# Cumulative sums of stick-breaking attention: six fp32 products for each head become six fp32r products on a split operand

## The chip, the cores and the metric

The kernel runs on one NeuronCore of a Trainium2 chip. The metric is the time of one execution on the device in microseconds (us). Its engines are named as in the profile: PE is TensorE (matmuls), PEld is TensorE's weight load, DVE is VectorE, ACT is ScalarE, POOL is GpSimd and SP is SyncE, whose queue issues most of the transfers.

## The reference, cut to what matters

The model is two transformer blocks on 256 tokens and 16 meta tokens. The change is inside the attention of the second block, in its eight stick-breaking heads. For each query the logarithm of the attention weight of a key is a log-sigmoid plus the sum of another log-sigmoid over all later keys, a reversed cumulative sum:

```
def stick_breaking_block(q, k, v, qpos, kpos):
    z = jnp.einsum('bhqd,bhkd->bhqk', q, k).astype(jnp.float32) * (SB_HEAD_DIM ** -0.5)
    causal = kpos[None, :] < qpos[:, None]
    u = jnp.where(causal, jax.nn.log_sigmoid(-z), 0.0)
    rest = lax.cumsum(u, axis=3, reverse=True) - u
    log_a = jax.nn.log_sigmoid(z) + rest
    a = jnp.where(causal, jnp.exp(log_a), 0.0)
    return jnp.einsum('bhqk,bhkd->bhqd', a.astype(v.dtype), v)
```

## The kernel before, in words

Nearly all of the work is a stream of weight units, each a 128x1024 piece of some weight matrix. A unit is loaded by SP (L130), and split into two fp32r tiles: ACT copies it to `hi` with rounding (L152) and DVE writes the remainder to `lo` (L154). `mm_w` then makes 24 products for it on PE (L183 to L185): high by high, high by low, low by high, for eight slices. Three `hi` and three `lo` buffers exist, so ACT may write the next `hi` when PE has done with the unit three before.

The second block begins, at 934 us of the span, with a transition: the sums of the expert layer are read from PSUM, normalised, transposed (`to_feats`) and become the operand `xT2` of all that follows. Then the eight stick-breaking heads run, from about 955 to 1053 us, and after them the eight heads of the differential attention. For each head `hd` three weight units give queries, keys and values (`ps_sq`, `ps_sk`, `ps_svT`). Between them, by hand, the steps of the generator `stick` are issued; each `yield` in it lets one more weight unit go by. So the attention of a head is spread over the units of the next two heads:

- Step 1: `z` is the product of keys and queries. Keys stand on the 128 partitions, in three tiles; queries stand in the columns. Of the 256 queries key tile 0 needs all, tile 1 only the last 144, tile 2 only the last 16, which makes 256 + 144 + 16 = 416 columns side by side in one PSUM bank. DVE adds the mask (L998), ACT makes the softplus in three steps (L1000 to L1002), and DVE ends it in `e` (L1003).
- Step 2, one unit later: the values are transposed (L985) and copied by ACT (L986).
- Step 3, two units later: the cumulative sums `S`, from `e`, on PE (L1011). For each key tile a product with the triangle `tri` sums the later keys of the same tile, and products with `ones` add all of the later tiles: tile 0 gets 256 columns from itself, 144 from tile 1 and 16 from tile 2; tile 1 gets 144 and 16; tile 2 gets 16. That makes six matmuls in fp32 and 592 columns. Each fp32 matmul stands in the trace as two records, with a weight load each. DVE subtracts `S` from `z` (L1013), and ACT takes the exponential (L1014).
- Step 4, two units later: the product with the values, `po` (L1019), which ACT and DVE split into `osb` (L1020, L1021).

The order on PE and SP is the program's. The order on ACT, DVE and POOL is set by a scheduler, by priority; each engine then runs its instructions strictly in that order.

Of the kernel before, what the change touches and what calls it, by code (L numbers as in the profile page):

```python
# [9 lines left out]
F32 = mybir.dt.float32  # L10
F32R = mybir.dt.float32r
I32 = mybir.dt.int32
U32 = mybir.dt.uint32
AF = mybir.ActivationFunctionType
ALU = mybir.AluOpType
# [4 lines left out]
P = 128  # L20
# [32 lines left out]
def two_blocks(ctx, tc, x, feats, vecs, w_in, w_out, w_q, keys, u, v, final_g, meta2, w_in2, lams, w_gate,  # L53
               w_br_sb, w_br_df, w_out2, w_fg, w_fu, w_fd, final_g2, gains, out):
    nc = tc.nc
# [9 lines left out]
    def phase(name):  # L65
        st = ExitStack()
        pool = st.enter_context(tc.tile_pool(name=name, bufs=1, reuse_waits="tile"))
        return st, pool

    def mm_tile(name):  # L70
        return pmm.tile([P, 512], F32, tag="mm", name=name)
# [3 lines left out]
    def at_tile(name):  # L75
        turn[0] += 1
        return pacc.tile([P, 512], F32, tag=f"a{turn[0] % 4}", name=name)
# [252 lines left out]
    ones = const.tile([P, P], F32, tag="ones", name="ones")  # L330
# [473 lines left out]
    for hd in range(NH):  # L804
        kt = pr.tile([P, 2, P], F32, tag="kt", name=f"kt{hd}", bufs=2)
        nc.sync.dma_start(kt, keys[:, 2 * hd:2 * hd + 2, :])
        qT = []
        for half in range(2):
            ps = mm_tile(f"q{hd}{half}")
# [118 lines left out]
    QN = [T - q0 for q0 in Q0]  # L928
    QO = [0, QN[0], QN[0] + QN[1]]
    NQ = sum(QN)  # L930
# [5 lines left out]
    s_sb, psb = phase("psb")  # L936
# [5 lines left out]
    for kt in range(3):  # L942
        o = mneg[:, QO[kt]:QO[kt] + QN[kt]]
        nc.gpsimd.affine_select(o, o, [[1, QN[kt]]], ALU.is_gt, -BIG, base=NM + Q0[kt] - kt * P, channel_multiplier=-1)
    tri = psb.tile([P, P], F32, tag="tri", name="tri")
    nc.gpsimd.affine_select(tri, ones, [[-1, P]], ALU.is_ge, 0.0, base=0, channel_multiplier=1)


    KN = [NM + P, L]
# [31 lines left out]
    def value(name, tag, vt):  # L981
        ps = at_tile(f"pv_{name}")
        o = psb.tile([P, 3, P], F32, tag=tag, name=name, bufs=2)
        for kt in range(3):
            nc.tensor.transpose(ps[:, kt * P:(kt + 1) * P], vt[:, kt * P:(kt + 1) * P], ident)  # L985
        nc.scalar.activation(o, ps[:, :KP].rearrange("p (a b) -> p a b", a=3), AF.Copy)  # L986
        return o

    def qcols(kt, j=None):
        j = kt if j is None else j  # L990
        return slice(QO[kt] + Q0[j] - Q0[kt], QO[kt] + QN[kt])

    def stick(hd, q, k, vT):
        pz = at_tile(f"z{hd}")
        for kt in range(3):
            nc.tensor.matmul(pz[:, qcols(kt)], k[:, kt * P:(kt + 1) * P], q[:, Q0[kt]:], start=True, stop=True)
        z = psb.tile([P, NQ], F32, tag="z", name=f"zs{hd}", bufs=2)
        nc.vector.tensor_tensor(z, pz[:, :NQ], mneg, op=ALU.add)  # L998
        e = psb.tile([P, NQ], F32, tag="e", name=f"e{hd}", bufs=2)
        nc.scalar.activation(e, z, AF.Abs)  # L1000
        nc.scalar.activation(e, e, AF.Exp, scale=-1.0)
        nc.scalar.activation(e, e, AF.Ln, bias=1.0)  # L1002
        nc.vector.scalar_tensor_tensor(e, z, 0.0, e, op0=ALU.max, op1=ALU.add)  # L1003
        yield
        vt = value(f"sv{hd}", "sv", vT)
        yield
        yield
        ps = at_tile(f"S{hd}")
        for kt in range(3):
            for j in range(kt, 3):  # L1010
                nc.tensor.matmul(ps[:, qcols(kt, j)], tri if j == kt else ones, e[:, qcols(j)],  # L1011
                                 start=(j == kt), stop=(j == 2))
        nc.vector.tensor_tensor(z, z, ps[:, :NQ], op=ALU.subtract)  # L1013
        nc.scalar.activation(z, z, AF.Exp)  # L1014
        yield
        yield
        po = at_tile(f"po{hd}")
        for kt in range(3):
            nc.tensor.matmul(po[:, Q0[kt]:T], vt[:, kt, :], z[:, qcols(kt)], start=(kt == 0), stop=(kt == 2))  # L1019
        nc.scalar.activation(osb[0][:, hd, :], po[:, :T], AF.Copy)  # L1020
        nc.vector.tensor_tensor(osb[1][:, hd, :], po[:, :T], osb[0][:, hd, :].bitcast(F32), op=ALU.subtract)  # L1021
# [73 lines left out]
    for hd in range(NH):  # L1095
        q = feat(f"sq{hd}", hd, "sq", QS, float(P) ** -0.5) if hd != 1 else ahead
        if hd > 1:
            q = q()
            advance()
        k = feat(f"sk{hd}", hd, "k", FULL, spare=(hd == 1))  # L1100
        if hd == 1:
            q = q()
            advance()
        if hd > 0:
            k = k()
            advance()
        else:
            with tc.high_priority(offset=20):
                cols = x2_norm()
        vT = feat(f"svT{hd}", hd, "vT", FULL)  # L1110
        if hd == 0:
            ahead = feat("sq1", 1, "sq", QS, float(P) ** -0.5)
            with first():
                across(pb, cols, rsb[:, QS], "rsb")
            tc.keep_in_program_order(nc.scalar.preload_act_table_set("natural_log_exp_and_others"))
            q, k = q(), k()
        running.append(stick(hd, q, k, vT()))
        if hd > 0:
            advance()
        if hd == 0:  # L1120
            with queued([latest["hi"], latest["lo"]]):
                small_parts()
# [8 lines left out]
    for m in range(16):  # L1131
        ps = mm_tile(f"g{m}")
# [13 lines left out]
    for m in range(KC):  # L1146
        ps = mm_tile(f"ysb{m}")
# [3 lines left out]
    for m in range(KC + 1):  # L1151
        if m < KC:
            ps = mm_tile(f"ydf{m}")
# [144 lines left out]
```

## Time and profile before

| | us |
|---|---|
| median of three runs | 1450.63 |
| lowest and highest | 1447.94 and 1456.06 |
| the profiled execution | 1450.2 |
| its span in the trace | 1448.2 |
| PE busy in the span | 1435.2 (99%) |
| DVE busy | 1049.0 (72%) |
| ACT busy | 743.4 (51%) |
| the stretch of the stick-breaking heads | 955 to 1053 |

The profiled execution took 2.0 us more than its span, for what lies around it. A busy PE in the table is a PE with a matmul in its pipeline; since matmuls overlap, their real cost is the distance from the start of one to the start of the next, and not their duration. Where a question is about one stage, the rows of that stage count, not the shares over the whole span.

### The profile page before, as it was taken

How to read it: one execution, taken by the hardware profiler on the slowest of the kernel's cores; microseconds unless marked ns; L12 is line 12 of the kernel's file. 1: busy time of each engine (PE TensorE's matmuls, PEld its weight loads, DVE VectorE, ACT ScalarE, POOL GpSimd, SP SyncE). 2: the span in 40 equal slices, each digit the busy share in tenths (PEclk: the TensorE clock that was granted, in tenths of full speed). 3: DMA queues.
4: the chain of work that ended last, by engine and by line, in shares of the span. 5: the costliest groups of instructions: out<-in, count | busy, mean ns of one | idle time of the engine just before them, and what ended most of it. 6: DMA issues, size and time to landing. Idle time of an engine off the chain costs nothing.

```text
span 1448.2 us, 25653 instructions
## 1 busy us (share of the span) xinstructions
PE 1435.2 (99%) x10150; PEld 1338.4 (92%) x10150; DVE 1049.0 (72%) x1887; ACT 743.4 (51%) x1236; POOL 15.5 (1%) x35
## 2 busy tenths in 40 slices
PE   9999999999999999999999999999999999999998
PEld 8988999999999999888888888899999999899997
DVE  8998789884998999655555565675577776765666
ACT  7556544544444444544444444564455764554444
POOL 0010000000000000000000000100000000000000
PEclk9999999999999999999999999999999999999999
DMA  7526656665444444566666676553434466556563
GB/s 245 197 80 197 195 179 181 183 200 184 153 132 146 147 141 139 183 194 192 194 196 192 192 254 191 182 181 117 131 117 132 131 183 183 173 185 192 186 195 102
DMA packets 69816, 248.96 MB, mean 172 GB/s; under 512 B 7744, under 2 KB 9152, under 8 KB 69696
## 3 DMA queue, kind: packets, MB, share of 16 engines
q1 hardware_dynamic: 68256, 242.61, 53.6%
q0 software_dynamic: 1152, 4.19, 0.9%
q8 instruction: 79, 1.29, 0.4%
q10 hardware_dynamic: 288, 0.52, 0.1%
q14 instruction: 41, 0.34, 0.1%
HBM read 245.20 MB, written 2.10 MB: 171 GB/s over the span
## 4 chain that ended last, share of the span: by engine, by line
PE 92%; DVE 5%; ACT 1%; issue 1%; DMA 0%; POOL 0%; SPq 0%; DVEq 0%; POOLq 0%; ACTq 0%
PE v L197 8%; PE v L199 8%; PE v L198 8%; PE u L183 7%; PE u L185 7%; PE u L184 7%; PE gp L753 4%; PE fg L184 1%; PE fg L185 1%; PE fg L183 1%; PE fu L183 1%; PE fu L185 1%; PE fu L184 1%; PE fd L199 1%; PE fd L198 1%; PE fd L197 1%
## 5 line engine op out<-in xcount | busy, mean ns | idle before, releaser
L154 DVE TENSOR_TENSOR lo<-raw,hi 128x1024 fp32r<-128x1024 f32 x453 | 552.1, 1224 | 244.0 <-ACT hi L152 241.7
L152 ACT ACTIVATE hi<-raw 128x1024 fp32r<-128x1024 f32 x453 | 477.0, 1058 | 420.4 <-PE u L184 119.8
L183 PE MATMUL u<-hThi,hi 128*128 128x256 f32 x1024 | 295.6, 289 | 0.0
L185 PE MATMUL u<-hThi,lo 128*128 128x256 f32 x1024 | 284.9, 278 | 0.6 <-DVE lo L154 0.6
L184 PE MATMUL u<-hTlo,hi 128*128 128x256 f32 x1024 | 284.8, 278 | 0.0
L198 PE MATMUL v<-lo,w_hi 128*128 128x512 f32 x512 | 199.3, 389 | 0.0
L199 PE MATMUL v<-hi,w_lo 128*128 128x512 f32 x512 | 199.2, 389 | 0.0
L197 PE MATMUL v<-hi,w_hi 128*128 128x512 f32 x512 | 199.2, 389 | 0.0
L185 PEld LDWEIGHTS u<-hThi,lo 128*128 128x128 f32 x1024 | 193.3, 189 | 1.2 <-DVE lo L154 1.2
L184 PEld LDWEIGHTS u<-hTlo,hi 128*128 128x128 f32 x1024 | 192.9, 188 | 0.0
L183 PEld LDWEIGHTS u<-hThi,hi 128*128 128x128 f32 x1024 | 192.7, 188 | 0.0
L198 PEld LDWEIGHTS v<-lo,w_hi 128*128 128x128 f32 x512 | 96.1, 188 | 20.2 <-DVE lo L154 0.2
L199 PEld LDWEIGHTS v<-hi,w_lo 128*128 128x128 f32 x512 | 96.1, 188 | 20.1
L197 PEld LDWEIGHTS v<-hi,w_hi 128*128 128x128 f32 x512 | 96.1, 188 | 19.6
L753 PE MATMUL gp<-ga,gb 128*128 128x128 f32 x512 | 74.9, 274 | 0.0
L753 PEld LDWEIGHTS gp<-ga,gb 128*128 128x128 f32 x512 | 66.2, 191 | 0.0
L851 ACT ACTIVATE w_hi<-ewa 128x512 fp32r<-128x512 f32 x48 | 30.4, 634 | 65.8 <-PE v L198 65.8
L853 DVE TENSOR_TENSOR w_lo<-ewa,w_hi 128x512 fp32r<-128x512 f32 x48 | 33.2, 693 | 38.6 <-ACT w_hi L851 38.6
L184 PE MATMUL fg<-hTlo,hi 128*128 128x256 f32 x176 | 48.9, 278 | 0.2 <-DVE hTlo L257 0.2
L183 PE MATMUL fg<-hThi,hi 128*128 128x256 f32 x176 | 48.9, 278 | 0.1
L185 PE MATMUL fg<-hThi,lo 128*128 128x256 f32 x176 | 48.9, 278 | 0.0
L183 PE MATMUL fu<-hThi,hi 128*128 128x256 f32 x176 | 48.7, 277 | 0.0
(417 smaller groups left out, 2957.7 us busy)
## 6 DMA issues: line engine op xcount, KB each, us to landing
raw<-in_u_dram SPq DMA_DIRECT2D x128, 512.0 KB, 3.6
raw<-in_v_dram SPq DMA_DIRECT2D x128, 512.0 KB, 3.6
raw<-in_w_in_dram SPq DMA_DIRECT2D x67, 512.0 KB, 3.6
raw<-in_w_fg_dram SPq DMA_DIRECT2D x22, 512.0 KB, 4.1
raw<-in_w_fu_dram SPq DMA_DIRECT2D x22, 512.0 KB, 3.5
raw<-in_w_fd_dram SPq DMA_DIRECT2D x22, 512.0 KB, 4.5
raw<-in_w_out_dram SPq DMA_DIRECT2D x16, 512.0 KB, 3.7
raw<-in_w_q_dram SPq DMA_DIRECT2D x16, 512.0 KB, 4.4
```

The costliest lines, as they stand in the source:

```text
L152: latest["hi"] = nc.scalar.activation(hi, loaded[i], AF.Copy)
L154: latest["lo"] = nc.vector.tensor_tensor(lo, loaded[i], hi.bitcast(F32), op=ALU.subtract)
L183: nc.tensor.matmul(ps, hi[:, ks], ahi[:, k, cols], start=(k == 0), stop=False)
L184: nc.tensor.matmul(ps, hi[:, ks], alo[:, k, cols], start=False, stop=False)
L185: nc.tensor.matmul(ps, lo[:, ks], ahi[:, k, cols], start=False, stop=(k == KC - 1))
L197: nc.tensor.matmul(ps, ahi[:, ts], hi[:, bs], start=first and n == 0, stop=False)
L198: nc.tensor.matmul(ps, ahi[:, ts], lo[:, bs], start=False, stop=False)
L199: nc.tensor.matmul(ps, alo[:, ts], hi[:, bs], start=False, stop=end)
L753: nc.tensor.matmul(p3[:, :, i], b[:, i, :], a[:, i, :], start=True, stop=True)
L851: nc.scalar.activation(hi, a, AF.Copy)
L853: nc.vector.tensor_tensor(lo, a, hi.bitcast(F32), op=ALU.subtract)
```

## The change

The operand `e` of the cumulative sums is split in two fp32r tiles: `ehi` is a rounded copy made by ACT, `elo` is the remainder, made by DVE. The constants `tri` and `ones` are copied once to fp32r by ACT (their values 0 and 1 are exact there). The six fp32 products of a head become six fp32r products, three for `ehi` and the same three for `elo`: one with the triangle over all 416 columns, which does the three tiles' own sums; one with `ones` that adds tile 1 to tile 0 (144 columns); and one with `ones` that adds tile 2 to both tile 0 and tile 1, by reading its 16 columns twice and writing them to two places of the bank (2 x 16 columns).

```
+    tri_r = psb.tile([P, P], F32R, tag="tri_r", name="tri_r")
+    nc.scalar.activation(tri_r, tri, AF.Copy)
+    ones_r = psb.tile([P, P], F32R, tag="ones_r", name="ones_r")
+    nc.scalar.activation(ones_r, ones, AF.Copy)
...
         nc.vector.scalar_tensor_tensor(e, z, 0.0, e, op0=ALU.max, op1=ALU.add)
+        ehi = psb.tile([P, NQ], F32R, tag="ehi", name=f"ehi{hd}", bufs=2)
+        nc.scalar.activation(ehi, e, AF.Copy)
+        elo = psb.tile([P, NQ], F32R, tag="elo", name=f"elo{hd}", bufs=2)
+        nc.vector.tensor_tensor(elo, e, ehi.bitcast(F32), op=ALU.subtract)
         yield
...
         ps = at_tile(f"S{hd}")
-        for kt in range(3):
-            for j in range(kt, 3):
-                nc.tensor.matmul(ps[:, qcols(kt, j)], tri if j == kt else ones, e[:, qcols(j)],
-                                 start=(j == kt), stop=(j == 2))
+
+
+        c0, c1 = qcols(0, 2).start, qcols(1, 2).start
+        o = 512 - 2 * (c1 - c0)
+        both = ps[:, o:].rearrange("p (a b) -> p a b", a=2)[:, :, c0 - o:c0 - o + QN[2]]
+        for half in (ehi, elo):
+            third = half[:, qcols(2)].unsqueeze(1).broadcast_to((P, 2, QN[2]))
+            nc.tensor.matmul(ps[:, :NQ], tri_r, half, start=(half is ehi), stop=False)
+            nc.tensor.matmul(ps[:, qcols(0, 1)], ones_r, half[:, qcols(1)], start=False, stop=False)
+            nc.tensor.matmul(both, ones_r, third, start=False, stop=(half is elo))
```

On PE the six products of head 4 stand where they stood, behind the values' unit of head 5 and ahead of `z` of head 5. Before:

```order
L185 MATMUL ps_svT_10856<-xT2hi,lo_10784 128x272
L1011 MATMUL S_10888<-e_10774,tri 128x256
L1011 MATMUL S_10888<-e_10774,ones 128x144
L1011 MATMUL S_10888<-e_10774,ones 128x16
L1011 MATMUL S_10888<-e_10774,tri 128x144
L1011 MATMUL S_10888<-e_10774,ones 128x16
L1011 MATMUL S_10888<-e_10774,tri 128x16
L996 MATMUL z_10897<-sq_10810,kpad_10103 128x256
```

and now:

```order
L185 MATMUL ps_svT_10880<-xT2hi,lo_10808 128x272
L1024 MATMUL S_10912<-ehi_10799,tri_r 128x416
L1025 MATMUL S_10912<-ehi_10799,ones_r 128x144
L1026 MATMUL S_10912<-ehi_10799,ones_r 128x2x16
L1024 MATMUL S_10912<-elo_10801,tri_r 128x416
L1025 MATMUL S_10912<-elo_10801,ones_r 128x144
L1026 MATMUL S_10912<-elo_10801,ones_r 128x2x16
L1000 MATMUL z_10921<-sq_10834,kpad_10107 128x256
```

Nothing else changes its place on PE; the 592 columns of a head are now 2 x 592.

On ACT and DVE the two new instructions of head 3 stand behind the split of weight unit 315, as in the other heads but the first. ACT:

```order
L1006 ACTIVATE e3_10661<-e3_10661 128x416
L152 ACTIVATE hi315_10712<-raw315_10615 128x1024
L1009 ACTIVATE ehi3_10666<-e3_10661 128x416
L990 ACTIVATE sv3_10704<-pv_sv3_10703 128x384
L152 ACTIVATE hi316_10750<-raw316_10671 128x1024
```

and DVE:

```order
L1007 SCALAR_TENSOR_TENSOR e3_10661<-zs3_10659,e3_10661 128x416
L154 TENSOR_TENSOR lo315_10714<-raw315_10615,hi315_10712 128x1024
L1011 TENSOR_TENSOR elo3_10668<-e3_10661,ehi3_10666 128x416
L980 SCALAR_TENSOR_TENSOR kpad0_10106<-ps_sk4_10709,rsb_10073 128x272
L154 TENSOR_TENSOR lo316_10752<-raw316_10671,hi316_10750 128x1024
```

The rows around them are those of before, in the same order. (In the first head `ehi0` stands ahead of the split of unit 308, and `elo0` behind `vTpad0`.)

At the transition into the second block the scheduler places the copies of the two constants on ACT, `ones_r` in the squares of the first sum and `tri_r` ahead of weight unit 301. Now:

```order
L950 ACTIVATE ones_r_10100<-ones_104 128x128
L216 ACTIVATE junk2_10016,r2_1_ss_10070<-ht1_10013 128x512
...
L253 ACTIVATE xT2hi_10020<-tr_x21_1_10057 128x4x128
L948 ACTIVATE tri_r_10098<-tri_10096 128x128
L152 ACTIVATE hi301_10121<-raw301_9950 128x1024
L152 ACTIVATE hi302_10125<-raw302_9969 128x1024
L216 ACTIVATE junk2_10016,r3_0_ss_10186<-x20_10024 128x512
L152 ACTIVATE hi303_10156<-raw303_9971 128x1024
```

Besides the two new rows, a square of `x20` has moved ahead of unit 303 there; on DVE one of the two halves of `x20` (L911) has moved from behind the low parts of units 301 and 302 to ahead of them. In the first head of the differential attention DVE takes some small steps in another order.

## Rows read from the trace of the kernel before

**Rows 1.** The page: busy time of the engines, and the chain that ended last, by engine.

```profile
PE 1435.2 (99%) x10150; PEld 1338.4 (92%) x10150; DVE 1049.0 (72%) x1887; ACT 743.4 (51%) x1236; POOL 15.5 (1%) x35
...
PE 92%; DVE 5%; ACT 1%; issue 1%; DMA 0%; POOL 0%; SPq 0%; DVEq 0%; POOLq 0%; ACTq 0%
```

**Rows 2.** The table of windows, for the stretch of the stick-breaking heads: its length, then busy time (and instructions) of PE, PEld, DVE, ACT and POOL, the granted clock as a share of full speed, the DMA engines' busy share, and GB/s.

```profile
955.00:1053.00 98.00, 98.00 (x774) 96.64 (x773) 54.91 (x86) 47.90 (x75) 0.00 (x0) 1.00 0.42 130
```

**Rows 3.** The chain that ended last, from 925 to 1075 us: start, length, and what. There are eight pieces of `S`, 1.50 us each but the second.

```profile
963.99 1.50 PE S L1011 x12
...
972.72 1.59 PE S L1011 x12
...
1048.32 1.50 PE S L1011 x12
```

**Rows 4.** The timeline of PE through the products of `S` of one head, in narrow windows, so that single records show their start (first column) and how long each was in the pipeline (second). Where a row says x2 or more, it holds the next records of that line too.

```profile
985.25 0.38 PE L1011 MATMUL S<-e,tri 128*128 128x256 f32 x1
...
985.68 0.29 PE L1011 MATMUL S<-e,ones 128*128 128x144 f32 x1
...
985.92 0.29 PE L1011 MATMUL S<-e,ones 128*128 128x16 f32 x2
985.95 0.26 PE L1011 MATMUL S<-e,ones 128*128 128x16 f32 x1
986.06 0.37 PE L1011 MATMUL S<-e,tri 128*128 128x144 f32 x1
...
986.64 0.26 PE L1011 MATMUL S<-e,tri 128*128 128x16 f32 x1
986.75 0.46 PE L996 MATMUL z<-sq,kpad 128*128 128x256 f32 x1
987.05 0.38 PE L996 MATMUL z<-sq,kpad 128*128 128x256 f32 x1
```

**Rows 5.** The same for the weight loads, in the same head: the first two are those of the 144-column triangle, the last two those of the first two fp32r products of the unit behind `z`.

```profile
986.03 0.19 PEld L1011 LDWEIGHTS S<-e,tri 128*128 128x128 f32 x1
986.15 0.19 PEld L1011 LDWEIGHTS S<-e,tri 128*128 128x128 f32 x1
...
987.63 0.19 PEld L183 LDWEIGHTS ps_sq<-xT2hi,hi 128*128 128x128 f32 x1
987.74 0.19 PEld L184 LDWEIGHTS ps_sq<-xT2lo,hi 128*128 128x128 f32 x1
```

**Rows 6.** The timeline of PE in fp32r units: the second and the last of 24 products with 256 columns, the second and the last of 24 with 272 columns, and five with 512 columns in a row, of which the first and the last stand here.

```profile
987.86 0.28 PE L184 MATMUL ps_sq<-xT2lo,hi 128*128 128x256 f32 x1
...
990.43 0.28 PE L185 MATMUL ps_sq<-xT2hi,lo 128*128 128x256 f32 x1
...
991.00 0.28 PE L184 MATMUL ps_sk<-xT2lo,hi 128*128 128x272 f32 x1
...
993.77 0.29 PE L185 MATMUL ps_sk<-xT2hi,lo 128*128 128x272 f32 x1
...
700.00 0.39 PE L197 MATMUL v<-hi,w_hi 128*128 128x512 f32 x1
...
700.91 0.39 PE L198 MATMUL v<-lo,w_hi 128*128 128x512 f32 x1
```

**Rows 7.** Groups of instructions by line, 955 to 1053 us: busy time, mean ns of one, idle time of the engine before them. One of ACT's 416-column steps.

```profile
L1001 ACT ACTIVATE e<-e 128x416 f32<-128x416 f32 x8 | 4.4, 554 | 0.3
```

**Rows 8.** The timelines of ACT, DVE and PE from `e` of head 3 to its `S`; in brackets the idle time ahead of an instruction and what ended it.

```profile
990.63 1.06 ACT L152 ACTIVATE hi<-raw 128x1024 fp32r<-128x1024 f32 x1 [0.23 <-PE ps_sq L184]
991.59 0.47 ACT L986 ACTIVATE sv<-pv_sv 128x384 f32<-128x384 f32 x1
993.98 1.06 ACT L152 ACTIVATE hi<-raw 128x1024 fp32r<-128x1024 f32 x1 [1.91 <-PE ps_sk L184]
...
991.09 0.58 DVE L1003 SCALAR_TENSOR_TENSOR e<-zs,e 128x416 f32<-128x416 f32 x1
991.72 1.23 DVE L154 TENSOR_TENSOR lo<-raw,hi 128x1024 fp32r<-128x1024 f32 x1
994.10 0.44 DVE L976 SCALAR_TENSOR_TENSOR kpad<-ps_sk,rsb 128x272 f32<-128x272 f32 x1 [1.16 <-PE ps_sk L185]
...
997.83 0.38 PE L1011 MATMUL S<-e,tri 128*128 128x256 f32 x1
```

**Rows 9.** The same for the first head: DVE's last step of `e`, DVE's next instruction, and PE's first product of `S`.

```profile
959.40 0.59 DVE L1003 SCALAR_TENSOR_TENSOR e<-zs,e 128x416 f32<-128x416 f32 x1 [0.78 <-ACT e L1002]
960.30 0.44 DVE L976 SCALAR_TENSOR_TENSOR vTpad<-ps_svT,rsb 128x272 f32<-128x272 f32 x1 [0.30 <-PE ps_svT L185]
...
963.83 0.59 PE L1011 MATMUL S<-e,tri 128*128 128x256 f32 x2
```

**Rows 10.** The timelines of ACT, DVE and PE at the transition: ACT's square of the first sum, with the idle time ahead of it, and the splits of units 301 and 302 (x2); DVE's low parts of 301 and 302 (x2) and the two halves of `x20`; PE's first product that reads the low part of 301.

```profile
936.94 0.63 ACT L216 ACTIVATE junk<-ht 128x512 f32<-128x512 f32 x1 [1.11 <-issue]
...
940.17 2.00 ACT L152 ACTIVATE hi<-raw 128x1024 fp32r<-128x1024 f32 x2
...
941.26 2.36 DVE L154 TENSOR_TENSOR lo<-raw,hi 128x1024 fp32r<-128x1024 f32 x2
943.54 1.29 DVE L911 TENSOR_TENSOR x<-ht,gb 128x512 f32<-128x512 f32 x2
...
943.79 0.29 PE L185 MATMUL ps_sk<-xT2hi,lo 128*128 128x272 f32 x1
```

## The prediction

> **What bounds the kernel now.** I read the page first. PE is busy for 99% of the span, and the chain that ended last runs over PE for 92% of it [rows 1]; so the end moves if PE gets less to do, or if PE is made to wait. Then the windows, since the change lies in one stage: from 955 to 1053 us PE is busy for all 98.00 us at a granted clock of 1.00 (its upper level, 2.4 GHz), while DVE has 54.91 and ACT 47.90 us of work there [rows 2]. Nothing waits longer than PE's own queue. The chain of waits agrees: the eight pieces of S lie in it with their whole length, 1.50 us seven times and 1.59 us once, in the second head, behind the short products of `po` [rows 3]. What PE saves in S therefore comes off the end one for one, as long as ACT and DVE have the new operands ready in time.
>
> **What a product costs on PE.** Durations overlap, so I take distances from start to start. Two things can set one. The first is the columns. In fp32r the rows show 22 distances in 2.57 us with 256 columns, 0.117 us each, 22 in 2.77 us with 272 columns, 0.126 us, and four in 0.91 us with 512, 0.2275 us [rows 6]. From 272 to 512 columns that is 0.42 ns for a column, and some 0.011 us for the product itself. In fp32 the pair of records of 256 columns takes 0.43 us (985.25 to 985.68), four times 0.42 ns a column, and the pair of 144 columns 0.24 us (985.68 to 985.92) [rows 4].
>
> The second is the weight load. Each record has its own, and consecutive loads never start closer than about 0.11 us: 986.03 and 986.15 in fp32, 987.63 and 987.74 in fp32r [rows 5]. A load runs beside the product before it, so it costs nothing behind a long product and shows behind a short one. The short ones of S prove it: the records of 16 columns need 16 x 4 x 0.42 ns = 0.03 us a pair, and the last record of S starts at 986.64 with `z` only at 986.75, 0.11 us later; and the first record of `z`, whose load had only just begun, takes 0.30 us (986.75 to 987.05) where the same shape takes 0.215 in S [rows 4]. That hole stays as it is, since S ends in short products before and after.
>
> **PE, the sum.** The removed block is 1.50 us for a head. The new block, walked through with the load rule (a load starts when the product before starts, and 0.11 us after the load before; a product streams when its load is done):
> - 416 columns on `tri_r`: its load hides behind the 272-column product ahead. Between 272 and 512 columns the rows give 0.126 + 144/240 x 0.1015 = 0.187 us.
> - 144 columns on `ones_r`: load hidden behind the 416 columns. 144 x 0.42 ns + 0.011 = 0.072 us; it starts at 0.187 and ends at 0.259.
> - 2 x 16 columns on `ones_r`: the load can start only at 0.187, and is done at 0.295; 0.014 us of columns and 0.011 bring the end to 0.32.
> - 416 columns of `elo`: load at 0.297, done at 0.405; end at 0.405 + 0.187 = 0.59.
> - 144 columns: end at 0.66; 2 x 16 columns: load at 0.59, done at 0.70; end at 0.72. `z` starts behind its own load, which can begin at 0.70, at about 0.73.
>
> So 0.73 in place of 1.50 us, 0.77 us less for a head and 8 x 0.77 = 6.2 us in all. The second head's 1.59 becomes 0.82 by the same rule, as the 0.09 us on top is the hole behind `po`.
>
> No row shows an fp32r product of under 256 columns, so the four short ones of a head are bounded from both sides. From below: no load shows at all, as between the two 16-column records at 985.92 and 985.95, 0.03 us apart [rows 4]. Then the block is 2 x (0.187 + 0.072 + 0.03) = 0.58 us, and the gain 8 x 0.92 = 7.4 us. From above: short products cost in fp32r what the rows show in fp32, 0.24 us for 144 columns, and 0.14 us for 16 (985.92 to 986.06) [rows 4], the 16 columns more put into its load. The block is then 2 x (0.187 + 0.24 + 0.14) = 1.13 us, and the gain 8 x 0.37 = 3.0 us. I take 0.73, because the loads of fp32r keep the same 0.11 us [rows 5], and the load is what decides the short products of S now. That the 2 x 16 columns are read twice and written to two places I cost at nothing: 32 columns need 0.014 us, and the load covers eight times that.
>
> **ACT and DVE.** ACT gets eight copies of 416 columns, 0.55 us each by the like step of `e` [rows 7], DVE eight subtractions of 416 columns, 0.58 us each by L1003 [rows 8]: 4.4 and 4.6 us, on engines that idle for 50 and 43 of these 98 us [rows 2]. What matters is lateness. In a steady head ACT ends the split of unit 315 at about 991.6, when `e` is nearly done (991.09 + 0.58 = 991.67), so `ehi` is there at 992.3. The copy of the values waits behind it, 0.6 us later than now; its reader is `po`, two units behind S. The next split is not reached before 993.98, after 1.91 us of idling for PE, so the delay ends there. DVE ends the low part of 315 at 992.95, and `elo` at 993.5; `kpad` behind it would have waited for PE until 994.10 anyway. PE reaches S at 997.83: `elo` is 4.3 us early [rows 8]. In the first head `e` ends at 959.99, `ehi` follows at 960.6, `elo` behind the 0.44 us of vTpad at 961.3, against PE's 963.83: 2.5 us early [rows 9]. The first product of a block waits for `ehi` on ACT and the fourth for `elo` on DVE, both long there, so I cost the new waits at nothing; without this cover each microsecond of lateness would cost a microsecond of PE, with everything queued behind it.
>
> **The transition.** The copies of the constants have 128 columns each, so each takes less than the 0.55 us of 416 columns [rows 7]. `ones_r` falls into 1.11 us in which ACT idles [rows 10]. `tri_r` shifts the splits of 301 and 302 by those 0.55 us at most, and DVE now does half of `x20` (1.29 / 2 = 0.64 us) ahead of the low part of 301. That part ends at 941.26 + 0.64 + 1.2 = 943.1 instead of 942.4, and PE reads it at 943.79 [rows 10]: 0.7 us to spare. Cost nothing; if the cover were gone, at most 0.64 + 0.55 = 1.2 us once. The few steps that DVE takes in another order in the first head of the differential attention I take at 0, with 0.3 us to either side.
>
> The sum: 1450.2 us of the profiled execution (1448.2 of span and 2.0 around it) less 6.2 is **1444.0 us**. The median of the three runs, 1450.63, lies 0.4 above that execution, within their scatter (1447.94 to 1456.06).
>
> **Rivals.**
> - Loads hide. The short products run at their columns' pace, the block is 0.58 us, and the time is 1450.2 - 7.4 = 1442.8. For it speaks the pair 0.03 us apart; against it, that the next one is again 0.11 us behind [rows 4]. The Trainium skill's page "TensorE: Matmul & The Clock Gate", section "Back-to-back issue gap", would put it there: it gives a lone product of up to 64 columns about 25 ns and no load. The trace agrees with that only where the load had already been made. Chance 0.15.
> - Short products stay dear. The fp32r pace of a column holds for long products alone; block 1.13 us, gain 3.0, time 1447.2. Nothing in the trace speaks against it directly, since every fp32r product there has 256 columns or more [rows 6]. Chance 0.2.
> - The gain does not arrive. S is shorter, but PE waits as much somewhere else, at the first products behind the transition or for `elo`: 1450. Against it stand 4.3, 2.5 and 0.7 us of cover [rows 8 to 10]. Chance 0.06.
> - Slower: `elo` comes late. PE takes its queue in order, so the fourth product of a block would hold up `z` of the next head and its units. The lateness would have to eat the 4.3 us of cover and the 0.77 us of gain before it costs anything, and 0.9 us more in every head for 0.5% of the time; that is a DVE 6 us behind. At 1 us more in each head the time is 1458. Chance 0.03.
>
> **How the numbers follow.** The forecast itself, 6.2 us or 0.43%, has 0.56. A measurement of this kernel tells about 0.5% (7.3 us) from no change, so the forecast lies just short of that line: with 0.1 or 0.2% of scatter some 0.3 of its own chance falls beyond it, and half of the first rival's; 0.56 x 0.32 + 0.15 x 0.55 = 0.26 for faster. Slower gets 0.04, the same 0.70. The range reaches from the first rival, with some 2 us of scatter below, to the second, with as much above: 1441 to 1449.
>
> **What would show it.** In the changed profile a piece of S in the chain should be 0.73 us (0.82 in the second head) and PE's busy time some 6 us less; 0.58 would speak for the first rival, 1.1 for the second. The stretch from the first S to the last should shrink from 84.3 by about 5.4 us (seven blocks). In the list of waits PE and PEld should not wait for `ehi` or `elo`. If S is as short as I say and the span is not 6 us shorter, the third rival is right, and the idle time of PE ahead of 955 or behind 1053 us shows where. An added wait of PE inside S, ahead of the fourth product, would make the whole prediction wrong.

## The result, and the profile after

| | before | changed |
|---|---|---|
| median, us | 1452.51 | 1444.18 |
| lowest and highest, us | 1447.94 and 1458.63 | 1441.74 and 1450.87 |
| runs | 8 | 8 |
| PE busy in the stretch from 955 to 1053 us | 98.00 of 98.00 | 98.00 of 98.00 |
| distance from the first `S` to the last, us | 84.33 | 79.1 |

The ratio is 0.9949, with a 95% interval from 0.9932 to 0.9965. Of 1452.5 us that is 7.4 us less, with 5.1 and 9.9 as the ends. The forecast was 1444.0 us. That it lies 0.2 us from the median of 1444.18 is in part luck: it started from 1450.2, and the median before, over eight runs, is 1452.5. What can be compared is the gain, 6.2 us forecast against 7.4.

The time says that something was gained, but not where. So the stage itself is read: PE's timeline through one block of `S` in the changed kernel, one record at a time, with start and time in the pipeline, from the block's first product to the two first records of `z` behind it:

```profile
998.04 0.35 PE L1024 MATMUL S<-ehi,tri_r 128*128 128x416 f32 x1
998.23 0.23 PE L1025 MATMUL S<-ehi,ones_r 128*128 128x144 f32 x1
998.30 0.23 PE L1026 MATMUL S<-ehi,ones_r 128*128 128x32 f32 x1
998.37 0.44 PE L1024 MATMUL S<-elo,tri_r 128*128 128x416 f32 x1
998.65 0.23 PE L1025 MATMUL S<-elo,ones_r 128*128 128x144 f32 x1
998.71 0.22 PE L1026 MATMUL S<-elo,ones_r 128*128 128x32 f32 x1
998.79 0.46 PE L1000 MATMUL z<-sq,kpad 128*128 128x256 f32 x1
999.09 0.38 PE L1000 MATMUL z<-sq,kpad 128*128 128x256 f32 x1
```

From 998.04 to 998.79 the block takes 0.75 us; before it took 1.50 [rows 4]. The weight loads of the same block, with the first load of `z` last:

```profile
998.04 0.19 PEld L1025 LDWEIGHTS S<-ehi,ones_r 128*128 128x128 f32 x1
998.23 0.19 PEld L1026 LDWEIGHTS S<-ehi,ones_r 128*128 128x128 f32 x1
998.34 0.19 PEld L1024 LDWEIGHTS S<-elo,tri_r 128*128 128x128 f32 x1
998.45 0.19 PEld L1025 LDWEIGHTS S<-elo,ones_r 128*128 128x128 f32 x1
998.65 0.19 PEld L1026 LDWEIGHTS S<-elo,ones_r 128*128 128x128 f32 x1
998.76 0.19 PEld L1000 LDWEIGHTS z<-sq,kpad 128*128 128x128 f32 x1
```

The two views belong together. Loads stand 0.11 us apart where they follow short products (998.23, 998.34, 998.45; 998.65, 998.76), and 0.19 or 0.20 where a product of 416 columns holds them up. The second product of 416 columns, at 998.37, needs 0.28 us to the next start where the first needs 0.19: its load began only at 998.34, 0.11 us behind the load before it. The hole of `z` is still there (0.30 us to its second record, as in [rows 4]).

The windows show the stage as before, PE full and its clock at the upper level, with more work on DVE and ACT (columns as in [rows 2]):

```profile
955.00:1053.00 98.00, 98.00 (x773) 96.51 (x772) 63.99 (x104) 55.19 (x89) 0.00 (x0) 1.00 0.45 139
```

DVE has 9.1 us more in it and ACT 7.3. The eight `elo` are 4.7 and the eight `ehi` 4.3 of that; the rest is other work, since the heads begin 2.4 us later in this execution and end 2.8 sooner. The new waits that could have come of it did not. This is the whole list of what PE waited for in the changed kernel, in us, times and longest; none of it is for `ehi` or `elo`:

```profile
PE gg L183 <- ACT xThi L346: 1.2, 1, 1.2
PE warm L338 <- DVE eps L333: 1.1, 1, 1.1
PE pss L530 <- POOL ysq L280: 1.1, 1, 1.1
PE x_ss L362 <- DVE sq L280: 0.8, 1, 0.8
PE q L185 <- DVE lo L154: 0.4, 1, 0.4
PE fg L184 <- DVE hTlo L257: 0.2, 1, 0.2
```

How long the operands lay ready is read from the timelines. The first row is `elo` of the head whose `S` begins at 998.04; the second and the third are `ehi` and `elo` of the first head, whose `S` begins at 966.27; the fourth is PE's first product that reads the low part of unit 301, and the fifth DVE's low parts of units 301 and 302:

```profile
993.47 0.59 DVE L1011 TENSOR_TENSOR elo<-e,ehi 128x416 fp32r<-128x416 f32 x1
...
962.47 0.55 ACT L1009 ACTIVATE ehi<-e 128x416 fp32r<-128x416 f32 x1 [0.66 <-DVE e L1007]
...
963.10 0.58 DVE L1011 TENSOR_TENSOR elo<-e,ehi 128x416 fp32r<-128x416 f32 x1
...
946.23 0.29 PE L185 MATMUL ps_sk<-xT2hi,lo 128*128 128x272 f32 x1
...
944.25 2.35 DVE L154 TENSOR_TENSOR lo<-raw,hi 128x1024 fp32r<-128x1024 f32 x2
```

`elo` ends at 994.06, 4.0 us ahead of the first product of `S` and 4.3 ahead of its own reader, the fourth. In the first head it ends at 963.68, 2.6 us ahead of the first product (2.9 of its reader), and `ehi` there at 963.02, 3.2 ahead. The low part of 301 is the first half of the last row, so it ends near 945.4, some 0.8 us ahead of the product that reads it.

One trap lies in this profile. Its execution took 1450.87 us, the longest of the eight, and its span of 1448.8 us is no shorter than the 1448.2 of before. The difference is not in the stage. The first square of the transition, before and now:

```profile
934.49 0.63 ACT L216 ACTIVATE junk<-ht 128x512 f32<-128x512 f32 x1 [1.89 <-DVE ht L897]
```

```profile
936.95 0.63 ACT L216 ACTIVATE junk<-ht 128x512 f32<-128x512 f32 x1 [1.89 <-DVE ht L897]
```

It begins 2.5 us later before any changed instruction has run. From there to the first `S`, through the two new copies, it is 29.34 us before and 29.32 now, so the transition costs nothing. From the start of the last `S` to the end it takes 403.4 us in place of 400.0. But for the last block itself, and the order of some small steps of DVE, that part holds the same work before and after; the same kernel run again (the last experiment) takes 399.3 there. So the distance from the first `S` to the last is the measure that one profile can give, and the medians are the other.

### The profile page after: what moved, and what is told of

Same layout as the page of the kernel before. It is cut to its first block, busy times and chain, and to the rows that moved or that the text cites. A ratio compares the mean times of both kernels' runs of the same rounds, so it can differ in the third digit from the quotient of the medians.

```text
span 1448.8 us, 25560 instructions
## 1 busy us (share of the span) xinstructions
PE 1436.4 (99%) x10102; PEld 1340.8 (93%) x10102; DVE 1053.2 (73%) x1895; ACT 746.2 (52%) x1246; POOL 15.5 (1%) x35
## 3 DMA queue, kind: packets, MB, share of 16 engines
q8 instruction: 79, 1.29, 0.4%
## 4 chain that ended last, share of the span: by engine, by line
PE 92%; DVE 5%; ACT 1%; issue 1%; DMA 0%; POOL 0%; SPq 0%; DVEq 0%; ACTq 0%; POOLq 0%
PE v L198 8%; PE v L197 8%; PE v L199 8%; PE u L183 7%; PE u L185 7%; PE u L184 7%; PE gp L753 4%; PE fg L184 1%; PE fg L185 1%; PE fu L185 1%; PE fu L184 1%; PE fu L183 1%; PE fg L183 1%; PE fd L199 1%; PE fd L198 1%; PE fd L197 1%
```

## The experiments

Theory A of the expectations is the prediction's load rule: a short product costs what its weight load costs. Theory B is that the columns decide, each at the pace of its type. Where an experiment asks something else, its text names its own rival. All edits are against the changed kernel unless it is said otherwise.

**The split alone.** The products stay as many as before, each once for `ehi` and once for `elo`, all in fp32r: twelve.

```
-        for half in (ehi, elo):
-            third = ...
-            nc.tensor.matmul(ps[:, :NQ], tri_r, half, ...)
...
+        for kt in range(3):
+            for half in (ehi, elo):
+                for j in range(kt, 3):
+                    nc.tensor.matmul(ps[:, qcols(kt, j)], tri_r if j == kt else ones_r, half[:, qcols(j)],
+                                     start=(half is ehi and j == kt), stop=(half is elo and j == 2))
```

> One part alone: e is split in two fp32r tiles, but the products stay unmerged, so a head has twelve fp32r products of 256, 144 and 16 columns in place of six. The columns are the same 2 x 592 as in the changed kernel. Theory A, the weight loads set the short products (0.11 us from load to load): walked through by that rule a block of S is 1.27 us, 0.23 less than before, 1.8 us less for the eight heads, so hardly a change of the time. Theory B, the columns set it: 1184 columns at 0.42 ns and 12 x 0.011 us are 0.63 us, less than the changed kernel's 0.75, and the time is some 7 us under before.

1451.63 us, ratio 0.9989 (0.9966 to 1.0011). In PE's timeline the block begins at 987.31 and `z` at 988.58, 1.27 us; its last three products, of 16 columns each, and `z`:

```profile
988.28 0.22 PE L1022 MATMUL S<-elo,ones_r 128*128 128x16 f32 x1
988.35 0.26 PE L1022 MATMUL S<-ehi,tri_r 128*128 128x16 f32 x1
988.47 0.26 PE L1022 MATMUL S<-elo,tri_r 128*128 128x16 f32 x1
988.58 0.68 PE L1000 MATMUL z<-sq,kpad 128*128 128x256 f32 x2
```

The last two products of 16 columns take 0.12 and 0.11 us to the next start, which is the distance of the loads. The one ahead of them takes 0.07, since its own load had begun earlier, at 988.21, when the product before it still ran. Theory A gave 1.27; by B the block would have been 0.63. So fp32r without fewer products saves 0.23 us of the 0.75.

**The merge alone**, in the kernel before: three fp32 products of 416, 144 and 2 x 16 columns, no split.

```
-        for kt in range(3):
-            for j in range(kt, 3):
-                nc.tensor.matmul(ps[:, qcols(kt, j)], tri if j == kt else ones, e[:, qcols(j)], ...)
+        third = e[:, qcols(2)].unsqueeze(1).broadcast_to((P, 2, QN[2]))
+        nc.tensor.matmul(ps[:, :NQ], tri, e, start=True, stop=False)
+        nc.tensor.matmul(ps[:, qcols(0, 1)], ones, e[:, qcols(1)], start=False, stop=False)
+        nc.tensor.matmul(both, ones, third, start=False, stop=True)
```

> The other part alone: the products are merged (416, 144 and 2 x 16 columns) but stay in fp32, with no split on ACT and DVE. Six records with six loads, as in the changed kernel, but four times the columns' pace on 592 columns. Theory A (loads set short products, columns long ones): block 1.09 us, 0.41 less than before, 3.3 us less for eight heads. Theory B (columns alone): 592 columns at four times 0.42 ns are 1.0 us both here and before, so before's 1.50 would have come from something else and nothing would be gained by merging: 1.50.

1449.95 us, ratio 0.9976 (0.9952 to 1.0001). PE's timeline, where each row holds the pair of records of one fp32 product, `z` last:

```profile
981.60 0.86 PE L1013 MATMUL S<-e,tri 128*128 128x416 f32 x2
982.30 0.41 PE L1014 MATMUL S<-e,ones 128*128 128x144 f32 x2
982.54 0.30 PE L1015 MATMUL S<-e,ones 128*128 128x32 f32 x2
982.68 0.68 PE L996 MATMUL z<-sq,kpad 128*128 128x256 f32 x2
```

The block is 1.08 us, where A gave 1.09 and B no gain. Merging alone saves 0.42 us a head. The two parts alone make 0.65, both together 0.75: they are not independent, and the likely reason, which was not tried by itself, is that the split doubles the products, which costs less the fewer short ones there are.

**The split without its use.** The constants, `ehi` and `elo` are made as in the changed kernel, but PE does the six fp32 products of before, on `e`. Nothing reads the two halves.

> The cost on ACT and DVE alone: the two constants and ehi and elo are made as in the changed kernel, but nothing reads them; PE does before's six fp32 products from e. The output is whole. My theory: the added 4.4 and 4.6 us hide in idle time, PE's list of waits stays as before, time the same within 1 us. Rival: they hold up the splits of the weights, and part of the gain of the changed kernel was eaten by it; then PE idles between 955 and 1053 us, and the time rises by 1 to 5 us.

1457.24 us, ratio 1.0020 (0.9998 to 1.0041): by its time alone this is open, since a loss of 0.2% lies just inside the interval. The chain of waits settles it for the stage:

```profile
971.62 1.50 PE S L1021 x12
...
1055.95 1.50 PE S L1021 x12
```

From the first to the last it is 84.33 us, to the hundredth what it was without the eight copies and eight subtractions [rows 3], and PE waits for nothing there. From the first square of the transition to the first `S` it is 29.34 us too, as before. What the profiled execution of 1462.05 us has more lies ahead of that square (it begins at 942.12 us, 7.6 later than before) and behind the last `S` (404.1 us to the end in place of 400.0), in code that is the same in both. Two executions of the changed kernel itself differ by as much in the second part, 403.4 and 399.3 us. So the rival's wait inside the stage is refuted; that the rest has nothing to do with the edit is argued from its place, and the median's 0.2% stays open.

**The new block five times.** Each head does its six products five times over, and keeps the last sums; 24 more products for a head on PE, nothing else.

```
-        for half in (ehi, elo):
+        for rep in range(5):
+            for half in (ehi, elo):
```

> The changed kernel with the six products of S issued five times in a row in every head (each time from a fresh start of the accumulation, so the sums are those of the last). Theory A, PE time in this stage comes off or on one for one, and each further block costs 0.81 us by the load rule (the long product's load no longer hides behind a unit): a block piece of 4.0 us, 8 x 3.25 = 26 us over the changed kernel, about 1470 us. Rival: part of what PE spends is hidden or given back elsewhere (weights that arrive late anyway, or waits behind 1053 us): less than 20 us.

1475.44 us, ratio 1.0164 (1.0121 to 1.0208): 23.8 us above before, and with the 7.4 us of the change 31 above the changed kernel, where the two intervals leave some 7 to either side. In the chain the repeats of one head follow each other like this (start, length; the long product of `elo`, of the next `ehi`, and of the next `elo`):

```profile
1038.44 0.29 PE S L1025
1038.86 0.28 PE S L1025
1039.27 0.29 PE S L1025
```

From `elo` to `elo` it is 0.83 us, where the load rule gave 0.81 for a block behind its like. 32 blocks of 0.83 are 26.5 us, and the 31 us, with 7 to either side, hold that: work on PE in this stage goes into the time one for one, as near as these intervals tell, and the rival's less than 20 us lies outside them.

**S one unit earlier.** One of the two units of distance between the values and `S` is taken out, so that PE comes for `ehi` and `elo` a unit sooner.

```
         yield
-        yield
         ps = at_tile(f"S{hd}")
```

> The changed kernel with the products of S issued one weight unit earlier (one yield of the generator less), so that a unit of 3.0 us of the cover of elo is gone. In the changed kernel's trace elo is ready 4.0 us ahead of S in a steady head (994.06 against 998.04) and 2.6 us in the first. Theory A, PE waits only for what is not ready: about 1 us of cover is left in the steady heads, so no wait there, at most 0.5 us in the first head, and the time of the changed kernel (0.995 of before). Rival, the cover is not what keeps PE from waiting (the split costs PE anyway): a wait on elo or ehi in every head.

1448.39 us, ratio 0.9974 (0.9951 to 0.9998), which overlaps the changed kernel's. In the list of PE's waits one row belongs to the stage:

```profile
PE S L1023 <- ACT ehi L1009: 0.4, 1, 0.4
```

It is the first head's, and it is for `ehi`, which the expectation had not priced: counted from the transition's first square PE came to `S` 3.6 us sooner there, and `ehi` had been 3.2 us early. In the steady heads PE waits for nothing, and the first records of `z` follow each other 11.79 us apart (975.73, 987.53, 999.32, 1011.11), where the changed kernel has 11.84. A cover of 4.0 us survives the loss of a unit of 2.7 to 3 us (`elo` is still 1.3 us ahead of `S` in the steady heads); the first head's does not, by 0.4 us.

**S two units earlier**: the second distance is taken out too.

> The same two units earlier, which is the rival of the prediction that ended slower, brought about on purpose. By theory A the cover is overdrawn: S stands right behind the transposes of the values, and elo comes some 2.6 us later than PE wants it, so PE waits that long in every head, 8 x 2.6 = 21 us more than the changed kernel, a ratio of about 1.009 to before, and the list of waits names elo's line. Theory C, waits for elo are given back because the weights' splits run ahead meanwhile and nothing else is late: less than 5 us.

1468.28 us, ratio 1.0108 (1.0074 to 1.0142); 21 us over the changed kernel was expected, which is 1.009, and by the two ratios of this chip (1.0108, and 0.9954 for the changed kernel run again) it is 22. The list of waits, and one block in PE's timeline with the idle time ahead of its products:

```profile
PE S L1022 <- ACT ehi L1009: 11.4, 8, 3.4
PE S L1022 <- DVE elo L1011: 5.2, 7, 0.7
```

```profile
989.33 0.46 PE L1022 MATMUL S<-ehi,tri_r 128*128 128x416 f32 x1 [1.29 <-ACT ehi L1009]
...
990.66 0.46 PE L1022 MATMUL S<-elo,tri_r 128*128 128x416 f32 x1 [0.74 <-DVE elo L1011]
```

PE idles twice in each block. The distance from the first `elo` product to the last grows from 79.1 to 99.93 us (963.77 to 1063.70 in the chain), 20.8 more. So the third and the fourth rival of the prediction are real where the cover is gone. That the sum met the 21 us is in part luck. A steady head grows from 11.84 to 14.30 us, 2.46 more, and the two waits are 2.03 of that, where 2.6 were expected from `elo` alone; two of the seven distances hold a stretch at the lower clock besides (last section). And most of the wait goes to ACT's copy, which comes first; only 5.2 of 16.6 us go to DVE's subtraction.

**Four products instead of six.** POOL adds up the later keys' columns beforehand: `late` holds, for tile 0, the 144 columns of tile 1 with the 16 of tile 2 added on, and for tile 1 the 16 of tile 2 behind 128 zeros. It is split into `lhi` and `llo` as `e` is, and one product with `ones_r` over 2 x 144 columns takes the place of the two short ones. That is more columns (2 x 704 for a head against 2 x 592) in fewer products; it also adds a copy on ACT and a subtraction on DVE in each head. `ehi` and `elo` have one buffer each there, instead of two.

```
+        nc.gpsimd.tensor_copy(late[:, 0, :], e[:, qcols(1)])
+        nc.gpsimd.tensor_copy(late[:, 1, QN[1] - QN[2]:], e[:, qcols(2)])
+        nc.gpsimd.tensor_tensor(late[:, 0, QN[1] - QN[2]:], late[:, 0, QN[1] - QN[2]:], e[:, qcols(2)], op=ALU.add)
+        nc.scalar.activation(lhi, late, AF.Copy)
+        nc.vector.tensor_tensor(llo, late, lhi.bitcast(F32), op=ALU.subtract)
...
-            nc.tensor.matmul(ps[:, qcols(0, 1)], ones_r, half[:, qcols(1)], start=False, stop=False)
-            nc.tensor.matmul(both, ones_r, third, start=False, stop=(half is elo))
+            nc.tensor.matmul(to, ones_r, l, start=False, stop=(half is elo))
```

> Fewer products with more columns. POOL adds the third key tile's e to the end of the second's, so that a single product with ones, 2 x 144 columns (the second half zero but for its last 16), serves both key tiles. A half is then 416 and 288 columns, four products for a head in place of six, and 1408 columns in place of 1184. Theory A (loads set short products): 288 columns need 0.133 us, more than a load, so no load shows any more: block 0.64 us in place of 0.75, and the hole behind it in z goes too, 0.81 in place of 0.90: 0.2 us less for a head, 1.6 us in all, 0.1% under the changed kernel. Theory B (columns): 224 columns more at 0.42 ns and two products less at 0.011, 0.07 us more for a head: 0.82.

1441.24 us, ratio 0.9922 (0.9896 to 0.9948). The block in PE's timeline:

```profile
992.19 0.35 PE L1032 MATMUL S<-ehi,tri_r 128*128 128x416 f32 x1
992.38 0.29 PE L1033 MATMUL S<-lhi,ones_r 128*128 128x288 f32 x1
992.51 0.35 PE L1032 MATMUL S<-elo,tri_r 128*128 128x416 f32 x1
992.70 0.30 PE L1033 MATMUL S<-llo,ones_r 128*128 128x288 f32 x1
992.83 0.97 PE L1003 MATMUL z<-sq,kpad 128*128 128x256 f32 x6
```

Both products of 416 columns now take 0.19 us, and the block 0.64 instead of 0.75, with 224 columns more. The load of `z` hides too: the piece of `z` in the chain shrinks from 0.90 to 0.80 us. Together that is 0.21 us a head, as theory A had it; by B the head would have become longer. The heads follow each other 11.63 us apart, 0.21 less than in the changed kernel.

**The changed kernel again**, beside the last three on the same chip.

> The changed kernel once more, beside the three above on the same chip: a ratio of 0.995 to before, S in pieces of 0.75 us, 79.1 us from the first S to the last. What differs from its first trace is the scatter of a run and not the change.

1444.03 us, ratio 0.9954 (0.9938 to 0.9970), and again 79.1 us from the first `S` to the last. This execution can be compared with that of before from the transition on, since the products behind the stage run at the same pace in both (0.1139 us, last section), which those of the changed kernel's first execution do not. Its first square of the transition:

```profile
937.88 0.63 ACT L216 ACTIVATE junk<-ht 128x512 f32<-128x512 f32 x1 [1.89 <-DVE ht L897]
```

From there to the end of the span of 1445.6 us it is 507.7 us, where it was 513.7 before (934.49 to 1448.2). That is 6.0 us less, eight times the 0.75 of a block: what `S` gives up arrives at the end whole. The version with four products is ahead by its median and in the stage, but the intervals of the two overlap: the order of the two is shown by the stage, not by the times.

## Why the prediction was right, step by step

- **The bound.** PE is full in the stage before and after. The 26.5 us that the repeats put on it came out as 31, with 7 to either side, and in the repeated run of the changed kernel the 6.0 us taken off it are gone from the transition's first square to the end. The step "what PE saves in S comes off the end one for one" held.
- **The block.** Forecast 0.73 us, measured 0.75. The walk by the load rule gave the six starts and that of `z` at 0, 0.187, 0.259, 0.32, 0.59, 0.66 and 0.73; they stand at 0, 0.19, 0.26, 0.33, 0.61, 0.67 and 0.75. The second head was to take 0.82 and takes 0.83 (974.27 to 975.10). The term was 0.02 us too small, spread over several products. So the gain in the stage is 8 x 0.75 = 6.0 us and not 6.2; the distance from the first `S` to the last shrank by 5.2 us and not by 5.4. The time's 7.4 us agree with both (5.1 to 9.9).
- **The first rival, loads that hide (0.58 us).** Refuted by the block of 0.75 us and by the loads' rows: no load starts closer than 0.11 us to the load before. Starts of products can stand 0.07 us apart (998.30 to 998.37), but then the next distance is longer (0.28 us in place of 0.19). The two records 0.03 us apart that spoke for this rival fit the load rule as well: the load of the first had begun at 985.80, 0.12 us ahead. The section "Back-to-back issue gap" of the Trainium skill's page "TensorE: Matmul & The Clock Gate" gives its 25 ns for an isolated product, without a load, and lets both set the pace in a stream of loads and products; so its 25 ns did not speak for 0.58 us in a block where every product brings its own load. Of the short products of `S` read here none is over sooner than 0.13 us after its own load began (0.14 from 998.23 to 998.37).
- **The second rival, short products that stay dear (1.13 us).** Refuted by the changed profile directly: a product of 144 columns takes 0.07 us in fp32r (998.23 to 998.30). It was the one case that the trace of before could not exclude.
- **The cover.** Forecast 4.3, 2.5 and 0.7 us; measured 4.0, 2.6 and 0.8. Unused halves cost PE nothing in the stage, one unit less of distance costs the first head 0.4 us, two cost the stage 20.8. So the zero in the sum was a hidden cost, and the distance in units is what hides it: one unit is enough in the steady heads, and the first head needs part of the second.
- **PE's busy time.** This step of "what would show it" failed: it was to be 6 us lower, and it is 1.2 higher, 1436.4, and in the repeated run 1.9 lower, 1433.3. The prediction treated a single execution's total as steady to much less than 6 us, and it is not (last section).

The prediction put its forecast just short of a line of 0.5%, and the result is as near to it: the interval of the ratio, 0.9932 to 0.9965, lies on both sides. The forecast's 0.43% and the 0.41% that 6.0 us make lie inside it.

## What to carry to other kernels

Count the short matmuls on PE, each with the distance of its weight load (0.11 us here), before counting their columns: a block is walked through start by start, and a change of type that doubles the products pays little by itself (0.23 us of 1.50 here) and more together with a merge that makes them few. Merging may even add columns, as long as each product is long enough to hide the next load. A zero for work on other engines is a statement on distance: read how early the operand is, and test it by moving the consumer closer until the wait shows.

## What the runs showed of the hardware that was not expected

**Two paces of the same product.** In code that no edit touches, the same fp32r products of 256 columns run at different distances in different executions, at a granted clock of 1.00 in each. The routing copies a `qT` every few us (ACT, L812), and the distance from one to the next but one repeats with its loop. In ACT's timeline of the kernel before, and then of the changed kernel:

```profile
166.29 0.36 ACT L812 ACTIVATE qT<-q 128x256 f32<-128x256 f32 x1
...
186.25 0.36 ACT L812 ACTIVATE qT<-q 128x256 f32<-128x256 f32 x1
```

```profile
168.00 0.36 ACT L812 ACTIVATE qT<-q 128x256 f32<-128x256 f32 x1
...
188.68 0.36 ACT L812 ACTIVATE qT<-q 128x256 f32<-128x256 f32 x1
```

That is 19.96 against 20.68 us; the products there start 0.1135 and 0.1178 us apart in the mean, from 150 to 200 us. From 1300 to 1400 us it is 0.1139 against 0.1178, and 0.1139 once more in the repeated run of the changed kernel. So the pace is not the edit's: one kernel shows both. From 150 to 200 us the block five times and the four products, which hold the edit, have 0.1135 as well. Differences of several us between totals fit this, while the stage repeats to a tenth. What sets the pace was not tried and stays open.

**A wait can cost more than its length.** With `S` two units earlier the mean granted clock from 955 to 1070 us is 0.94, where it is 1.00 in the stage of the kernel before and of the changed one. The windows of that kernel (columns as in [rows 2]), around the first head and around the fifth, and its chain show where, and the pace in it:

```profile
955.00:970.00 15.00, 11.61 (x68) 11.27 (x67) 6.87 (x14) 6.75 (x11) 0.00 (x0) 0.77 0.41 121
...
1012.00:1026.00 14.00, 11.98 (x82) 11.58 (x81) 6.43 (x11) 5.98 (x10) 0.00 (x0) 0.88 0.36 111
```

```profile
1020.79 0.23 PE ps_sk L183
1021.01 0.23 PE ps_sk L184
```

In the first head PE had waited 3.39 us for `ehi`, and the block of `S` and most of the unit behind it run slowly, to about 969.3. In the fifth head, behind waits of 1.29 and 0.73 us, the products of 272 columns follow each other 0.23 us apart instead of 0.126 [rows 6] from about 1020.6 to 1023.9: that is the lower level of TensorE's clock, 1.2 GHz. The eighth head has such a stretch too (a granted clock of 0.79 from 1062 to 1070 us). In the third, fourth, sixth and seventh heads waits of the same length were followed by none (1.00 from 970 to 1012, from 1026 to 1042 and from 1042 to 1062 us), so which waits bring it was not settled.
